# Both parts of every weight tile written by DMAs instead of by ScalarE and VectorE

## The chip, the cores and the metric

One core of a Trainium2 chip runs the whole program. The metric is the device time of one execution in microseconds. Two runs of the kernel before took 2135.54 and 2133.32 us, a median of 2134.43 us.

## The reference

The reference is a decoder trunk of two layers over 512 tokens of width 1024, in float32, with a memory of 256 tokens. Each layer adds, to the running `x`, half of a SwiGLU FFN (inner width 2816), a token mixer, a cross-attention with four heads into the memory, and half of a second FFN. An RMS norm stands ahead of each step and one at the end.

```
x = x + 0.5 * swiglu_ffn(rms_norm(x, ffn1_norm[i]), ...)
x = x + mixer_i(rms_norm(x, mix_norm[i]))
x = x + memory_cross_attention(rms_norm(x, xattn_norm[i]), rms_norm(mem, mem_norm[i]), ...)
x = x + 0.5 * swiglu_ffn(rms_norm(x, ffn2_norm[i]), ...)
```

The mixer of layer 0 is a causal pooling over 2, 4, 8 and 16 positions with a small linear map per channel group. The mixer of layer 1 is a native sparse attention (NSA): 16 heads in 4 groups, with a compressed branch, a selected branch and a sliding window.

## The kernel before

**Number format.** Every product is worked out in float32r, to which a float32 value is rounded first. So that nothing is lost, each operand is held as a pair: a high part, which is the value rounded to float32r, and a low part, which is the value minus the high part. `mm3` (lines 274 to 278) multiplies two pairs with three matmuls: high by high, high by low, low by high. Where the weight is the first operand, the third of these matmuls (L278) is the first that reads its low part; where it is the second operand (the values of the memory and the keys and values of NSA), it is the second one (L277).

**The weights.** All weights, 192 MB, lie in one array in the order of their use, cut into 741 tiles of 128 partitions by at most 512 columns (719 of them full, 256 KB each). A full tile mostly holds four blocks of 128 by 128. Each block is used for one `mm3`, 512 tokens wide in the FFNs, the projections of `x` and the output projections, and 256 memory tokens wide for the keys of the memory (`mem_k`). In `mem_v` a whole tile is one block, used for two `mm3`. The reading side, `take` (from L257), asks at the first block of tile t that `split` has been called for the tiles up to t + AHEAD.

**How a tile is prepared.** `Stream.load` (L235) lets SyncE (SP) load it into a raw buffer. `Stream.split` lets ScalarE (ACT) round it into the high part (L246). `Stream.low` lets VectorE (DVE) subtract the high part from the raw tile (L255); during NSA, from `use_pool` on, GpSimd (POOL) does this for the odd tiles. There are 4 raw buffers and 5 buffers for pairs. A pair's buffer is free when the last matmul of the tile in it has ended.

**Order.** The stages run in the order of the reference. The last output products of one stage run beside the norm and the first products of the next. The memory's norm and preparation run beside the output products of the first FFN; `mem_k`, `mem_v` and the pooling mixer share a stage, and the memory of layer 1 is projected beside the end of NSA. A scheduler orders the instructions on each engine by its own costs, with the calls' order as priority, and adds the semaphore waits. So an engine's order isn't always that of the calls: ACT rounds tiles up to four ahead of their use, and ahead of work that was called earlier. Each engine, and each queue of an engine that issues DMAs, works in its own order.

Of the kernel before, what the change touches and what calls it, by code (L numbers as in the profile page):

```python
# [13 lines left out]
P = 128  # L14
# [29 lines left out]
WT = 512  # L44
# Units of a head's softmax run this many units ahead of their values.
LAG = 3
# Units at which the four steps of the next group's compressed branch are issued (from 16: in the next group).
CMP = (12, 15, 16, 18)
# Units of the last group but one at which a quarter of the memory is prepared.
MP = (12, 13, 14, 15)  # L50
# Where in the k order of the first products a norm is worked out: FFN, cross-attention, NSA (columns, row).
NORMS = (3, 6, 3, 7)
# The pool mixer beside the memory's projections, by step: the norm (a, b), the windows' sums on GpSimd (f) and their
# means (m), or both on the vector engine (n).
HOOKS = "10:a 12:b 16:f4 16:f5 20:n0 24:n1 31:f6 40:n2 42:m4 48:f7 48:n3 58:m5 68:m6 73:m7"
# Products that keep the tensor engine's clock up while the first loads are under way.
WARM = 8
# Steps of other projections done by the end of each unit of a group.
FILL = ([3, 3, 3, 6, 9, 14, 16, 17, 18, 21, 23, 24, 24, 24, 24, 24],
# [138 lines left out]
def plan():  # L198
    """The weights in the order of their use, cut into tiles of up to WT columns."""
    tiles, cur, n, off = [], [], 0, 0  # L200
    for s in all_segs():
        if s is None or n + s[3] > WT:
            tiles.append((cur, off, n))
            off += P * n
            cur, n = [], 0
        if s is None:
            continue
        cur.append(s)
        n += s[3]
    tiles.append((cur, off, n))  # L210
    return tiles, off + P * n
# [6 lines left out]
class Stream:  # L218
    """The weights in the order of their use: each tile is loaded once and split into two float32r
    parts whose sum is the tile exactly."""  # L220

    RAW, HL, AHEAD = 4, 5, 3

    def __init__(self, nc, dram, raw_pool, hl_pool):
        self.nc, self.dram, self.raw_pool, self.hl_pool = nc, dram, raw_pool, hl_pool
        self.where = [(t, j) for t, (segs, _, _) in enumerate(TILES) for j in range(len(segs))]
        self.pos = 0
        self.raw, self.hl = [], []
        self.use_pool = False

    def load(self, n):
        while len(self.raw) < min(n, len(TILES)):
            _, off, w = TILES[len(self.raw)]
            r = self.raw_pool.tile([P, WT], F32, name="wraw")
            self.nc.sync.dma_start(r[:, :w], bass.AP(tensor=self.dram.tensor, offset=self.dram.offset + off,  # L235
                                                     ap=[[w, P], [1, w]]))
            self.raw.append(r)

    def split(self, n):
        while len(self.hl) < min(n, len(TILES)):  # L240
            self.load(len(self.hl) + self.RAW)
            t = len(self.hl)
            w = TILES[t][2]
            pool = self.kept_pool if t >= len(TILES) - KEPT else self.hl_pool
            self.hl.append(pool.tile([P, 2, WT], F32R, name="whl"))
            self.nc.scalar.copy(self.hl[t][:, 0, :w], self.raw[t][:, :w])  # L246
            if t > 0:
                self.low(t - 1)
            if t == len(TILES) - 1:
                self.low(t)  # L250

    def low(self, t):
        w, hl = TILES[t][2], self.hl[t]
        eng = self.nc.gpsimd if self.use_pool and t % 2 else self.nc.vector
        eng.tensor_sub(hl[:, 1, :w], self.raw[t][:, :w], hl[:, 0, :w].bitcast(F32))  # L255

# [12 lines left out]
class Kernel:  # L269
# [10 lines left out]
    def mm4(self, ps, a, b, start, stop, **kw):  # L280
        """Contraction over stacked parts: a holds both parts of one side, b each part of the other."""
        mm = self.nc.tensor.matmul
        mm(ps, a, b[0], start=start, stop=False, **kw)
        mm(ps, a, b[1], start=False, stop=stop, **kw)

    def split(self, hl, src):
        """hl: the pair of float32r parts of src."""
        self.nc.scalar.copy(hl[0], src)
        self.nc.vector.tensor_sub(hl[1], src, hl[0].bitcast(F32))
# [15 lines left out]
    def run(self):  # L305
        tc, nc = self.tc, self.nc
        pool = tc.tile_pool
        with pool(name="const", bufs=1) as const, pool(name="tmps", bufs=5) as self.tmps, \
                pool(name="small", bufs=4) as self.small, pool(name="bc", bufs=1) as self.bc, \
                pool(name="xg", bufs=DK) as self.xgp, \  # L310
                pool(name="raw", bufs=Stream.RAW) as rawp, pool(name="hl", bufs=Stream.HL) as hlp, \
                pool(name="psum", bufs=8, space=bass.MemoryType.PSUM) as self.psum:
            self.const = const
            self.ws = Stream(nc, self.wts, rawp, hlp)
            self.identf = const.tile([P, P], F32, name="identf")
# [47 lines left out]
    def gained(self, k, g):  # L363
        """x[k] * gain as two parts."""
        nc = self.nc
# [7 lines left out]
    def squared(self, k, eng=None):  # L373
        """The share of x[k] in the norm's sum."""
        nc = self.nc
# [8 lines left out]
    def stage_x(self, k, g, eng=None):  # L384
        """What the next norm and its products need of x[k], once it is final."""
        if g is not None:
            if k == 0:
                self.xg = [None] * DK
            self.gained(k, g)
        self.squared(k, eng)  # L390

    def rms_cols(self, sums, nt, tag):
        """1/rms by token as columns [128, nt]."""
        nc = self.nc
# [11 lines left out]
    def spread(self, rcol, nt):  # L406
        """The columns as a row on every partition, in PSUM."""
        pb = self.bank("psb")
# [9 lines left out]
    def rms_row(self, row, hl, more=None):  # L418
        """1/rms by token as a row on every partition, from the parts of its sum (and a further one in float32)."""
        nc = self.nc  # L420
# [19 lines left out]
    def first(self, pss, outs, xs, k0=0, k1=DK, hooks=None):  # L440
        """Several outputs at once, so that the last of xs are needed late."""
        for k in range(k0, k1):
# [73 lines left out]
    def finish(self, outs, hT):  # L516
        """The last products and the final norm; the last output goes by halves of the tokens, so that the first
        half is normalised and stored beside the products of the second."""
        nc = self.nc
# [61 lines left out]
    def mem_norm(self):  # L581
        """The memory by its 1/rms, on every partition."""
        nc = self.nc
# [18 lines left out]
    def mem_prep(self, l):  # L602
        """The normalised memory as two parts."""
        nc = self.nc
# [19 lines left out]
    def mem_k(self, l, hd):  # L624
        """K^T of a head: kT[head] is the pair of parts, [128, chunk of the head's width, key]."""
        nc = self.nc
# [13 lines left out]
    def mem_v(self, l):  # L640
        """V: v[key block][half of the width] is the pair of parts."""
        nc = self.nc
# [18 lines left out]
    def pool_sums(self, k):  # L661
        """x[k] over its rms, and its sums over the trailing window (for a window of two: the token before, and for
        the first token that token itself)."""
        nc, att = self.nc, self.att
# [17 lines left out]
    def pool_means(self, k, h, s, rc, half):  # L682
        """The trailing means minus the token itself, times the gain, as two parts."""
        nc = self.nc
# [174 lines left out]
    def nsa(self, gnext):  # L859
# [62 lines left out]
        def blocks(kv):  # L922
            """The blocks of 32 positions as columns: [position % 2 and channel, position // 2, group and block]."""
            kc = [self.b8("kc").rearrange("p (c n) -> p c n", c=16) for _ in range(2)]
# [48 lines left out]
        def cmp_k(hT):  # L973
            """Keys by group, between columns of zeros."""
            ps = self.bank("psk")
# [13 lines left out]
        def cmp_v(hR, w):  # L989
            """Values by group, with the rows of the other heads' blocks at zero for each head."""  # L990
            w = [[t[:, None, :].to_broadcast([P, 2, P]) for t in wc] for wc in w]
# [170 lines left out]
        def begin(u):  # L1162
            """The scores of a unit, and the softmax of the one before."""
            if 0 <= u - 1 < len(units):
                normalised(*units[u - 1], *pr[u - 1])
            if u < len(units):
                pr[u] = softmax(*units[u])
# [105 lines left out]
def pack(inputs):  # L1273
    """The weights as one array in the order of their use, and the small arrays by partition."""
    mats = {}
# [46 lines left out]
```

## Time and profile before

| | |
|---|---|
| runs shown | 2133.32 and 2135.54 us, median 2134.43 us |
| span of the profiled execution, first to last instruction | 2132.6 us, 1.8 us under the median of the runs; its time outside the span is not shown |
| TensorE matmul (PE) | 2103.2 us busy, 99% of the span |
| VectorE (DVE) | 1186.2 us, 56% |
| ScalarE (ACT) | 916.9 us, 43% |
| GpSimd (POOL) | 237.8 us, 11% |
| DMA | 200.57 MB in all, mean 94 GB/s |

Busy time is the time in which an engine works on an instruction; DMA-issuing instructions are not counted in it. Matmuls overlap, so the time from the start of one to the start of the next tells more than the duration of one. The granted clock of TensorE is in the profile as a share of its full speed, 2.4 GHz.

### The profile page before, as it was taken

The numbers are of one execution on the slowest core, as the hardware profiler recorded it, in microseconds if no ns is written. First come the engines' busy times: TensorE is split into PE (matmuls) and PEld (weight loads), VectorE is DVE, ScalarE is ACT, GpSimd is POOL, SyncE is SP. The second block draws the span as 40 slices with busy tenths as digits, with TensorE's granted clock in tenths as the row PEclk, the third lists the DMA queues.
The fourth block names the chain that finished last, engine by engine and source line by source line (L and its number), as shares of the span: only waits on it lengthen the run. The fifth ranks groups of instructions, "written<-read, shape, count | busy, mean of one in ns | idle before, by whom it ended". The sixth has DMA issues, their size and how long they took to land.

```text
span 2132.6 us, 27926 instructions
## 1 busy us (share of the span) xinstructions
PE 2103.2 (99%) x10144; PEld 1769.6 (83%) x10144; DVE 1186.2 (56%) x2049; ACT 916.9 (43%) x1748; POOL 237.8 (11%) x294
## 2 busy tenths in 40 slices
PE   9999999899999999999999999999999999999998
PEld 6888888788888888888888888888898888888887
DVE  7554444964645453455544336788986555454433
ACT  4333333464533333343333334887876444333332
POOL 2000000511000000000000003544453100000000
PEclk9999999899999999999999999999999999999999
DMA  4333333431333333333333332411224223333332
GB/s 139 109 99 97 116 94 99 121 113 56 96 97 99 97 96 99 94 99 95 98 97 96 99 96 78 129 36 45 61 59 132 86 72 96 95 98 99 95 99 80
DMA packets 111035, 200.57 MB, mean 94 GB/s; under 512 B 12464, under 2 KB 17328, under 8 KB 110896
## 3 DMA queue, kind: packets, MB, share of 16 engines
q1 hardware_dynamic: 110208, 198.20, 31.8%
q8 instruction: 80, 1.31, 0.3%
q10 hardware_dynamic: 688, 0.58, 0.1%
q14 instruction: 59, 0.48, 0.1%
HBM read 196.63 MB, written 2.10 MB: 93 GB/s over the span
## 4 chain that ended last, share of the span: by engine, by line
PE 93%; DVE 3%; ACT 2%; issue 1%; DMA 1%; POOL 0%; DVEq 0%; SPq 0%; ACTq 0%; POOLq 0%
PE psy L277 10%; PE psy L276 10%; PE psy L278 10%; PE psu L277 7%; PE psg L277 7%; PE psg L278 7%; PE psu L278 7%; PE psu L276 7%; PE psg L276 7%; PE pso L1142 2%; PE psq L278 2%; PE psq L277 2%; PE psq L276 2%; PE pst L1130 1%; PE psf L278 1%
## 5 line engine op out<-in xcount | busy, mean ns | idle before, releaser
L246 ACT CAST whl<-wraw 128x512 fp32r<-128x512 f32 (+2 forms) x741 | 455.1, 617 | 901.9 <-PE psy L278 284.1
L255 DVE TENSOR_TENSOR whl<-wraw,whl 128x512 fp32r<-128x512 f32 (+1 forms) x687 | 483.2, 705 | 513.5 <-ACT whl L246 508.3
L276 PE MATMUL psy<-hT,whl 128*128 128x512 f32 (+1 forms) x726 | 278.0, 383 | 0.0
L278 PE MATMUL psy<-hT,whl 128*128 128x512 f32 (+1 forms) x726 | 277.8, 383 | 0.0
L277 PE MATMUL psy<-hT,whl 128*128 128x512 f32 (+1 forms) x726 | 277.8, 383 | 0.0
L277 PE MATMUL psu<-xg,whl 128*128 128x512 f32 x640 | 249.0, 389 | 0.0
L276 PE MATMUL psu<-xg,whl 128*128 128x512 f32 x640 | 249.0, 389 | 0.0
L276 PE MATMUL psg<-xg,whl 128*128 128x512 f32 x640 | 249.0, 389 | 0.0
L278 PE MATMUL psg<-xg,whl 128*128 128x512 f32 x640 | 249.0, 389 | 0.0
L278 PE MATMUL psu<-xg,whl 128*128 128x512 f32 x640 | 249.0, 389 | 0.0
L277 PE MATMUL psg<-xg,whl 128*128 128x512 f32 x640 | 249.0, 389 | 0.0
L255 POOL TENSOR_TENSOR whl<-wraw,whl 128x512 fp32r<-128x512 f32 (+2 forms) x54 | 70.1, 1298 | 849.3 <-ACT whl L246 840.5
L278 PEld LDWEIGHTS psy<-hT,whl 128*128 128x128 f32 x726 | 136.4, 188 | 26.8
L276 PEld LDWEIGHTS psy<-hT,whl 128*128 128x128 f32 x726 | 136.4, 188 | 26.6
L277 PEld LDWEIGHTS psy<-hT,whl 128*128 128x128 f32 x726 | 136.4, 188 | 26.4
L276 PEld LDWEIGHTS psu<-xg,whl 128*128 128x128 f32 x640 | 120.2, 188 | 25.2
L276 PEld LDWEIGHTS psg<-xg,whl 128*128 128x128 f32 x640 | 120.1, 188 | 25.1
L278 PEld LDWEIGHTS psg<-xg,whl 128*128 128x128 f32 x640 | 120.2, 188 | 24.8
L277 PEld LDWEIGHTS psg<-xg,whl 128*128 128x128 f32 x640 | 120.1, 188 | 24.9
L277 PEld LDWEIGHTS psu<-xg,whl 128*128 128x128 f32 x640 | 120.1, 188 | 24.8
L278 PEld LDWEIGHTS psu<-xg,whl 128*128 128x128 f32 x640 | 120.1, 188 | 24.8
L469 DVE TENSOR_TENSOR u<-psu,rbc 128x512 f32<-128x512 f32 x80 | 55.3, 692 | 103.1 <-PE psu L278 103.1
(291 smaller groups left out, 3417.7 us busy)
## 6 DMA issues: line engine op xcount, KB each, us to landing
wraw<-wts SPq DMA_DIRECT2D x719, 256.0 KB, 2.6
wraw<-wts SPq DMA_DIRECT2D x12, 192.0 KB, 2.4
x<-xT SPq DMA_DIRECT2D x8, 256.0 KB, 5.6
mraw<-memT SPq DMA_DIRECT2D x4, 512.0 KB, 4.2
out<-y SPq DMA_DIRECT2D x6, 256.0 KB, 3.6
wraw<-wts SPq DMA_DIRECT2D x8, 152.0 KB, 2.2
out<-y ACTq DMA_DIRECT2D x2, 256.0 KB, 3.6
wraw<-wts SPq DMA_DIRECT2D x2, 128.0 KB, 2.2
```

Of the source, the lines that this page charges most:

```text
L246: self.nc.scalar.copy(self.hl[t][:, 0, :w], self.raw[t][:, :w])
L255: eng.tensor_sub(hl[:, 1, :w], self.raw[t][:, :w], hl[:, 0, :w].bitcast(F32))
L276: mm(ps, a[0], b[0], start=start, stop=False)
L277: mm(ps, a[0], b[1], start=False, stop=False)
L278: mm(ps, a[1], b[0], start=False, stop=stop)
L469: nc.vector.tensor_mul(u, psu, self.rbc)
L1130: nc.tensor.transpose(pt[:, j * P:(j + 1) * P], pr[br][:, j * P:(j + 1) * P], self.identf)
L1142: nc.tensor.matmul(ps[:, c0:c0 + 256], v[br][j][:, g, :], pT[br][:, hl, j, :], start=False, stop=br == 1 and j == 2 * i2 + 1 and hl == 1)
```

## The change

The raw buffers, SP's loads, ACT's rounding copy and the subtraction on DVE and POOL are gone. In their place a DMA issued by POOL loads the tile from float32 into the high part, whose type is float32r. ACT writes the negative of the high part into the low part. A second DMA issued by POOL reads the same tile again and adds it to what stands in the low part (`accum_op`). There are 7 buffers for pairs in place of 5 and 4 raw ones, which is the same memory. `split` keeps 2 tiles ahead in place of 3, and the first DMA of a tile is called 2 further tiles ahead. Everything else, the matmuls too, is as before; the rest of the diff removes comments.

```diff
-    RAW, HL, AHEAD = 4, 5, 3
+    RAW, HL, AHEAD = 3, 7, 2
...
     def load(self, n):
-        while len(self.raw) < min(n, len(TILES)):
-            _, off, w = TILES[len(self.raw)]
-            r = self.raw_pool.tile([P, WT], F32, name="wraw")
-            self.nc.sync.dma_start(r[:, :w], bass.AP(...))
-            self.raw.append(r)
-
-    def split(self, n):
         while len(self.hl) < min(n, len(TILES)):
-            self.load(len(self.hl) + self.RAW)
             t = len(self.hl)
             w = TILES[t][2]
             pool = self.kept_pool if t >= len(TILES) - KEPT else self.hl_pool
             self.hl.append(pool.tile([P, 2, WT], F32R, name="whl"))
-            self.nc.scalar.copy(self.hl[t][:, 0, :w], self.raw[t][:, :w])
-            if t > 0:
-                self.low(t - 1)
-            if t == len(TILES) - 1:
-                self.low(t)
-
-    def low(self, t):
-        w, hl = TILES[t][2], self.hl[t]
-        eng = self.nc.gpsimd if self.use_pool and t % 2 else self.nc.vector
-        eng.tensor_sub(hl[:, 1, :w], self.raw[t][:, :w], hl[:, 0, :w].bitcast(F32))
+            self.nc.gpsimd.dma_start(self.hl[t][:, 0, :w], self.src(t))
+
+    def split(self, n):
+        while self.done < min(n, len(TILES)):
+            self.load(self.done + self.RAW)
+            t = self.done
+            w, hl = TILES[t][2], self.hl[t]
+            self.nc.scalar.mul(hl[:, 1, :w], hl[:, 0, :w].bitcast(F32), -1.0)
+            self.nc.gpsimd.dma_start(hl[:, 1, :w], self.src(t), accum_op=ALU.add)
+            self.done += 1
```

## Rows read from the trace of the kernel before

**Rows 1.** The page's busy times of the engines and the span.
```profile
span 2132.6 us, 27926 instructions
PE 2103.2 (99%) x10144; PEld 1769.6 (83%) x10144; DVE 1186.2 (56%) x2049; ACT 916.9 (43%) x1748; POOL 237.8 (11%) x294
```

**Rows 2.** Waits of PE: who waited for whom, total us, times, longest us.
```profile
PE psv L277 <- DVE whl L255: 5.6, 2, 4.4
PE psk L278 <- DVE whl L255: 4.6, 3, 2.9
PE psf L278 <- DVE whl L255: 2.8, 2, 2.4
```

**Rows 3.** The page's groups of instructions that prepare the weights.
```profile
L246 ACT CAST whl<-wraw 128x512 fp32r<-128x512 f32 (+2 forms) x741 | 455.1, 617 | 901.9 <-PE psy L278 284.1
L255 DVE TENSOR_TENSOR whl<-wraw,whl 128x512 fp32r<-128x512 f32 (+1 forms) x687 | 483.2, 705 | 513.5 <-ACT whl L246 508.3
...
L255 POOL TENSOR_TENSOR whl<-wraw,whl 128x512 fp32r<-128x512 f32 (+2 forms) x54 | 70.1, 1298 | 849.3 <-ACT whl L246 840.5
```

**Rows 4.** ACT's instructions in time, 1002 to 1008 us, in the second layer's first FFN.
```profile
1002.21 0.62 ACT L246 CAST whl<-wraw 128x512 fp32r<-128x512 f32 x1 [1.41 <-PE psu L278]
1004.93 0.62 ACT L246 CAST whl<-wraw 128x512 fp32r<-128x512 f32 x1 [2.10 <-PE psu L278]
1006.91 0.62 ACT L288 CAST hT<-u 128x512 fp32r<-128x512 f32 x1 [1.36 <-DVE u L470]
1007.65 0.62 ACT L246 CAST whl<-wraw 128x512 fp32r<-128x512 f32 x1
```

**Rows 5.** Stretches: PE, PEld, DVE, ACT, POOL busy (count), PEclk, DMA share, GB/s.
```profile
900.00:1100.00 200.00, 200.00 (x884) 165.59 (x883) 101.08 (x146) 72.03 (x114) 0.00 (x0) 1.00 0.34 97
370.86:432.77 61.91, 52.71 (x302) 46.78 (x300) 56.11 (x83) 29.11 (x50) 26.81 (x20) 0.89 0.44 128
```

**Rows 6.** Stretches, L246 alone: ACT busy (count), PEclk, DMA share, GB/s.
```profile
370.00:433.00 63.00, 19.72 (x32) 0.89 0.44 128
1370.00:1600.00 230.00, 24.23 (x40) 1.00 0.17 49
1610.00:1636.00 26.00, 10.69 (x18) 1.00 0.58 178
```

**Rows 7.** A stretch, PE alone: PE busy (count), PEclk, DMA share, GB/s.
```profile
392.00:396.00 4.00, 4.00 (x20) 0.50 0.48 134
```

**Rows 8.** PE's high-by-high matmuls in time, in `mem_k`, then `mem_v`.
```profile
381.16 0.28 PE L276 MATMUL psk<-mg,whl 128*128 128x256 f32 x1
381.52 0.28 PE L276 MATMUL psk<-mg,whl 128*128 128x256 f32 x1
...
421.21 0.39 PE L276 MATMUL psv<-whl,mg 128*128 128x512 f32 x1
421.89 0.39 PE L276 MATMUL psv<-whl,mg 128*128 128x512 f32 x1
```

**Rows 9.** DMA: the whole span's load issues; then 6 to 10 us.
```profile
wraw<-wts SPq DMA_DIRECT2D x719, 256.0 KB, 2.6
DMA to landing us min/median/max: 2.0/2.6/5.7
...
DMA packets 768, 1.40 MB, mean 350 GB/s; under 512 B 84, under 2 KB 84, under 8 KB 768
q1 hardware_dynamic: 768, 1.40, 97.6%
```

**Rows 10.** One DMA issue on SP's queue and two POOL groups, as durations.
```profile
1.25 0.42 SPq L235 DMA_DIRECT2D wraw<-wts  x1
...
L670 POOL TENSOR_TENSOR hp<-x,rbc 128x512 f32<-128x512 f32 x4 | 6.4, 1616 | 8.3 <-ACT rbc L438 8.3
L485 POOL TENSOR_TENSOR sqsum<-x 128x512 f32<-128x512 f32 x1 | 1.0, 1038 | 2.8 <-DMA x<-xT 2.8
```

**Rows 11.** PE in time at the opening: first and last low-part wait.
```profile
6.93 0.62 PE L278 MATMUL psf<-xg,whl 128*128 128x512 f32 x2
...
20.67 0.50 PE L278 MATMUL psf<-xg,whl 128*128 128x512 f32 x1 [2.41 <-DVE whl L255]
```

More of the change, by code (lines that the diff above doesn't have):

```diff
@@ L218, with __init__, src @@
 class Stream:
-    RAW, HL, AHEAD = 4, 5, 3
-    def __init__(self, nc, dram, raw_pool, hl_pool):
-        self.nc, self.dram, self.raw_pool, self.hl_pool = nc, dram, raw_pool, hl_pool
+    RAW, HL, AHEAD = 3, 7, 2
+    def __init__(self, nc, dram, hl_pool):
+        self.nc, self.dram, self.hl_pool = nc, dram, hl_pool
         self.where = [(t, j) for t, (segs, _, _) in enumerate(TILES) for j in range(len(segs))]
         self.pos = 0
-        self.raw, self.hl = [], []
+        self.hl, self.done = [], 0
         self.use_pool = False
+    def src(self, t):
+        _, off, w = TILES[t]
+        return bass.AP(tensor=self.dram.tensor, offset=self.dram.offset + off, ap=[[w, P], [1, w]])
     def load(self, n):
-        while len(self.raw) < min(n, len(TILES)):
-            _, off, w = TILES[len(self.raw)]
-            r = self.raw_pool.tile([P, WT], F32, name="wraw")
-            self.nc.sync.dma_start(r[:, :w], bass.AP(tensor=self.dram.tensor, offset=self.dram.offset + off,
-                                                     ap=[[w, P], [1, w]]))
-            self.raw.append(r)
-    def split(self, n):
         while len(self.hl) < min(n, len(TILES)):
-            self.load(len(self.hl) + self.RAW)
             t = len(self.hl)
@@ L310, in run @@
                 pool(name="xg", bufs=DK) as self.xgp, \
-                pool(name="raw", bufs=Stream.RAW) as rawp, pool(name="hl", bufs=Stream.HL) as hlp, \
+                pool(name="hl", bufs=Stream.HL) as hlp, \
                 pool(name="psum", bufs=8, space=bass.MemoryType.PSUM) as self.psum:
             self.const = const
-            self.ws = Stream(nc, self.wts, rawp, hlp)
+            self.ws = Stream(nc, self.wts, hlp)
             self.identf = const.tile([P, P], F32, name="identf")
```

## The prediction

> **What bounds the kernel now.** I read the busy times first: PE works 2103.2 of 2132.6 us, so all its idle time is 29.4 us, while DVE is at 56% and POOL at 11% [rows 1]. The next view is who PE waits for. Three rows of low parts that DVE had not finished (L255) hold 13.0 us of that idle time [rows 2]. After such a stall the granted clock is the lower level, 1.2 GHz, for some microseconds: 0.50 in a stretch of 4 us [rows 7]. The stretch of `mem_k`, `mem_v` and the pooling mixer shows what this costs: 32 tiles are rounded for it [rows 6]; its 16 tiles of `mem_k` need four blocks of 0.36 us each, its 16 tiles of `mem_v` two of 0.68 us [rows 8], so 16 x 1.44 + 16 x 1.36 = 44.8 us, and it takes 61.9 us at a mean clock of 0.89 [rows 5]. That is a loss of 17.1 us. Elsewhere PE is full: 200.0 us of 200 in an FFN, at clock 1.00, with a DMA share of 0.34 [rows 5].
>
> So DVE's 483.2 us of subtractions [rows 3] are work beside PE. The question is whether two DMAs for each tile keep up with PE. In the FFNs PE takes one tile in 1004.93 - 1002.21 = 2.72 us [rows 4]. This is the budget of POOL's queue and of the DMA engines for a tile.
>
> **What is removed.** 687 subtractions on DVE at 705 ns and 54 on POOL at 1298 ns [rows 3], 553.3 us of busy time, all of it covered by PE except for the waits above. ACT's 741 casts of 617 ns become 741 multiplications of the same shape; ACT has 57% of the span idle [rows 1], so I cost them at nothing. If each took 0.1 us more, that would be 74 us, still under PE. SP's 741 loads go too, and with them SP's wait for a raw buffer. The cost of issuing moves to POOL.
>
> **What is added: DMA work.** With the queue full, the engines move 350 GB/s at 97.6% of their time, so one pass over a tile of 262,144 bytes takes 0.75 us [rows 9]. At the present spacing a pass takes 0.34 x 2.72 = 0.92 us of share [rows 5]. The first DMA is one pass. The accumulating one is not in the trace. At the least it is one pass more, 1.50 us for the tile. It must also read what it adds to: three passes, 2.25 us. With a further pass for writing it is four, 3.0 us, or 4 x 0.92 = 3.68 us at the dearer rate, the upper bound. I take 2.25 us, since the rate of the full queue is nearest to a state in which the engines hardly rest: 83% of 2.72, covered in the FFNs. The Trainium skill, page "Collectives: The Full Stack", section "The bandwidth ceiling: the fold count and why AG ≠ RS ≠ AR", says that an add in the DMA path costs a second source read and not the add itself; by it the tile would be at three passes, 2.25 us, without it 1.50. No row here shows such a transfer.
>
> **What is added: POOL issues.** There are 1482, two per tile. SP spends 0.42 us on one [rows 10], which is the lower bound: 0.84 us for a tile. The upper bound is the slowest POOL operation on a whole tile, 1.62 us, 3.24 us for a tile. I take POOL's fast one, 1.04 us [rows 10], between the two ends: 2.08 us, under the budget. The Trainium skill, page "DMA: Bandwidth & Descriptors", section "Latency and other measured facts", gives about 1 µs to the first byte for a DMA issued by GpSimd and 0.6 for one issued by SP; an estimate of 2 x 1 us from it stays in the budget too. No row here shows one.
>
> **The wait that is added, and its queue.** The accumulating DMA waits on POOL for ACT's negation, and that waits for the first DMA to land. By the order of the calls three tiles' loads are ahead, so the loop from one load over its negation to the next is: landing 2.6 us [rows 9] + 0.62 + two issues at 1.04 = 5.3 us, and the budget of three tiles is 8.2 us. Behind the waiting instruction on POOL are the next loads and, in NSA, the scaling of the probabilities; there only 40 tiles are prepared in 230 us [rows 6], 5.8 us each. Seven pair buffers leave six tiles, 16.3 us, for two landings and a negation, 5.8 us in all, so latency alone is hidden. ACT's order helps: it rounds one tile just before and one just after an FFN activation without losing the beat of 2.72 us [rows 4].
>
> **Where tiles are short, it is not covered.** In the stretch of 61.9 us, with four tiles ready on entry, the stream sets (32 - 4) x 2.25 = 63.0 us: +1.1 us. DVE's backlog no longer matters there, but the stream takes its place. With 1.50 us PE's own 44.8 us remain (-17.1), with 3.0 us it is 84 us (+22). The second `mem_v`, 16 tiles at 1.36 = 21.8 us with 18 casts in its 26 us [rows 6], would take (16 - 4) x 2.25 = 27.0 us: +5.2. At the opening the first low part is used at 6.93 us [rows 11]; now it needs a second landing after the first. One landing of 2.6 us more, against 0.7 us of a subtraction, is about +2 us; a stall of 2.41 us at 20.67 [rows 11] and its slow clock may go in return. I take +2, with bounds of -4 and +6.
>
> **The sum.** 1.1 + 5.2 + 2 = +8.3 us on the span of 2132.6, or 2140.9; the runs' median lies 1.8 us above this span, hence **2143 us**. With two passes the same stages give -17.1 + 0 - 4 = -21: 2113 us.
>
> **The rivals.**
> - **The stream is slower than PE in the FFNs** (slower than before). It decides from 2.72 us a tile on, either by the DMA passes or by POOL's issues. Of the 741 tiles some 640 lie outside the three stretches of rows 6 and the opening. Each 0.1 us above the budget costs 64 us. With 3.0 us: 640 x 0.28 + 22 + (12 x 3.0 - 21.8 = 14) + 6 = +221, 2355 us. With POOL at 3.24 us: 640 x 0.52 + 29 + 17 + 6 = +385, 2519 us. At 3.68: 614 + 41 + 22 + 6 = +683, 2817 us. For it: no row prices either DMA, both issue on one engine, and three passes at the present spacing's 0.92 us are 2.76 us, just above the budget. Against it: the full queue's 350 GB/s, and POOL's idle time in the FFNs (0.00 busy in 200 us [rows 5]).
> - **POOL's queue order** (slower, just). If a landing takes 5.7 us, the longest in the trace [rows 9], the loop of three tiles is 5.7 + 0.62 + 2.08 = 8.4 us, 2.80 a tile: 640 x 0.08 = +51 and the +8, 2194 us. For it: transfers queue behind each other at 83% share. Against it: the median of 2.6 us.
> - **Faster by more than 2%**, under 2092 us: not even 29.4 us of PE's idle time suffice, and the slow clock would have to go as well. Nothing in the rows gives it beyond that.
>
> **Chances.** Covered in the FFNs, 2113 to 2177 us: 0.47, the likeliest. Stream bound: 0.41. Queue order: 0.10. Faster: 0.01; something else: 0.01. What a measurement of this kernel can tell from no change is about 2%, 43 us. So faster 0.01, within 2% 0.48 (0.47 and the near end of the queue's case), slower 0.51. The likeliest case's own range is 2108 to 2177; since slower cases hold half of the chance, the range that should hold 8 in 10 goes up to 2640, about 3.4 us a tile, with some 0.16 above and little below.
>
> **What would show it.** Right: PE still near 99% with a tile per 2.72 us in the FFNs, a DMA share near 0.83, no waits on low parts there, and the stretch with the mixer ending on waits for `whl` by DMA rather than by DVE. Wrong: PE waiting for the second DMA in each FFN tile, at 1.2 GHz after each stall. Then the DMA share tells the rivals apart: near 1, the passes are dearer than 0.75 us; well under 1 with POOL's queue issuing all the time, it is the issues; with POOL waiting for ACT, the order. A share near 0.55 would say two passes.

## The result, and the profile after

The changed kernel took 2632.86 and 2665.11 us, median 2648.99, against 2134.43 before: a ratio of 1.2413, with a 95% interval of 1.2233 to 1.2592. The forecast was 2143 us, so it failed, and the time lies 9 us above the upper end of the range too. The profiled execution is the one of 2632.86 us.

The page of the kernel after (L243 is the first DMA of a tile, L250 the negation, L251 the accumulating DMA):

```profile
span 2631.2 us, 28798 instructions
PE 2282.5 (87%) x10144; PEld 1764.4 (67%) x10144; DVE 722.1 (27%) x1362; ACT 902.3 (34%) x1748; POOL 1208.9 (46%) x1722
...
q0 software_dynamic: 213408, 384.79, 74.7%
...
L251 POOL DMA_DIRECT2D whl<-wts x741 | 656.5, 895 | 1244.5 <-ACT whl L250 1182.2
L250 ACT ACTIVATE whl<-whl 128x512 fp32r<-128x512 f32 (+2 forms) x741 | 463.6, 627 | 1604.7 <-DMA whl<-wts 1543.6
L243 POOL DMA_DIRECT2D whl<-wts x741 | 630.3, 863 | 66.8 <-PE psy L275 28.9
```

Set beside [rows 1]: the span grew by 498.6 us. PE's idle time went from 29.4 to 348.7 us, and its busy time from 2103.2 to 2282.5 us for the same 10144 matmuls; the mean granted clock fell from 0.994 to 0.977, which makes some 37 of these 179 us (an estimate: 2103.2 x (0.994 / 0.977 - 1)); the rest of them is not explained here. DVE lost its subtractions (1186.2 to 722.1 us), and nothing came of that. The weight DMAs hold the engines for 74.7% of the span; that this is not all they can do is seen in runs below, where the share goes up to 1.14. The line that tells the story is L251's: POOL stood idle for 1182.2 us ahead of accumulating DMAs, waiting for ACT.

Waits of the kernel after (who waited for whom, total us, times, longest us):

```profile
ACT whl L250 <- DMA whl<-wts: 1543.6, 636, 6.4
POOL whl L251 <- ACT whl L250: 1182.2, 620, 5.2
...
PE psy L275 <- DMA whl<-wts: 81.5, 118, 2.6
...
PE psu L275 <- DMA whl<-wts: 63.6, 90, 1.7
PE psg L275 <- DMA whl<-wts: 54.8, 79, 2.5
```

Read from below: PE's first matmul that needs a low part (L275, before it was L278) waits for a DMA; the accumulating DMA waits for the negation; the negation waits for the first DMA. All three happen in the FFNs, where [rows 5] had PE full. The same kind of stretch now (PE, PEld, DVE, ACT, POOL busy (count), PEclk, DMA share, GB/s):

```profile
1100.00:1300.00 200.00, 171.94 (x697) 129.65 (x695) 39.26 (x56) 55.69 (x91) 82.94 (x117) 0.97 0.78 153
```

In 200 us there are 697 matmuls where [rows 5] has 884, so a tile takes 2.72 x 884 / 697 = 3.45 us. The DMA share is 0.78, under the 1.02 that `e_order3` reaches below with PE full, so the engines are not what limits. POOL's queue in this stretch shows why (start us, us, engine, line, operation, idle time before it and what ended it):

```profile
1203.31 0.89 POOL L243 DMA_DIRECT2D whl<-wts  x1
1205.02 0.86 POOL L251 DMA_DIRECT2D whl<-wts  x1 [0.83 <-ACT whl L250]
1205.57 0.88 POOL L243 DMA_DIRECT2D whl<-wts  x1
1209.95 0.86 POOL L251 DMA_DIRECT2D whl<-wts  x1 [3.51 <-ACT whl L250]
1210.50 0.89 POOL L243 DMA_DIRECT2D whl<-wts  x1
1211.81 0.86 POOL L251 DMA_DIRECT2D whl<-wts  x1 [0.43 <-ACT whl L250]
1212.36 0.89 POOL L243 DMA_DIRECT2D whl<-wts  x1
1217.01 0.86 POOL L251 DMA_DIRECT2D whl<-wts  x1 [3.77 <-ACT whl L250]
```

And ACT's negations there:

```profile
1209.03 0.63 ACT L250 ACTIVATE whl<-whl 128x512 fp32r<-128x512 f32 x1 [4.30 <-DMA whl<-wts]
...
1210.89 0.63 ACT L250 ACTIVATE whl<-whl 128x512 fp32r<-128x512 f32 x1 [0.72 <-DMA whl<-wts]
1216.09 0.63 ACT L250 ACTIVATE whl<-whl 128x512 fp32r<-128x512 f32 x1 [4.57 <-DMA whl<-wts]
```

Two things are to be seen. First, loads and accumulating DMAs alternate. How far apart they are is told by counting them from the start to 1206 us (POOL busy (count), PEclk, DMA share, GB/s; L243 alone, then L251 alone):

```profile
0.00:1206.00 1206.00, 311.29 (x359) 0.97 0.80 158
```

```profile
0.00:1206.00 1206.00, 315.57 (x357) 0.97 0.80 158
```

The 359th load, at 1205.57 us, was issued right behind the 357th accumulating DMA. So when POOL waits to accumulate into tile c, only one further load, that of c+1, is under way; the load of c+2 stands behind the waiting instruction. In the order of the calls it stands ahead of it; the scheduler's order on POOL is another.

Second, the load that left at 1205.57 us released ACT at 1210.89: 5.3 us, twice the 2.6 us of a load before [rows 9]. Each load follows directly on an accumulating DMA. The loop is thus load, 5.3 us to the negation, 0.63 for it, 0.3 to the next accumulating DMA (1211.81), 0.55 to the next load (1212.36): 6.8 us, in which two tiles are fetched. The neighbouring loop takes 1217.01 - 1209.95 = 7.1 us. Half of it is the 3.45 us for a tile found above.

### The profile page after: what moved, and what is told of

It reads as the page before. It is cut to its first block, busy times and chain, and to the rows that moved or that the text cites. A ratio compares the mean times of both kernels' runs of the same rounds, so it can differ in the third digit from the quotient of the medians.

```text
span 2631.2 us, 28798 instructions
## 1 busy us (share of the span) xinstructions
PE 2282.5 (87%) x10144; PEld 1764.4 (67%) x10144; DVE 722.1 (27%) x1362; ACT 902.3 (34%) x1748; POOL 1208.9 (46%) x1722
## 3 DMA queue, kind: packets, MB, share of 16 engines
q0 software_dynamic: 213408, 384.79, 74.7%
## 4 chain that ended last, share of the span: by engine, by line
issue 46%; POOL 33%; PE 8%; DMA 8%; DVE 2%; ACT 2%; POOLq 0%; SPq 0%; ACTq 0%; DVEq 0%
POOL whl L243 19%; POOL whl L251 12%; DMA whl<-wts 8%; PE pso L1139 1%; ACT whl L250 1%; PE pst L1127 1%; PE psy L275 1%; PE psy L274 1%; PE psy L273 1%; POOL pr L1120 1%; PE psq L275 0%; POOL prx L793 0%; PE psq L273 0%; PE psq L274 0%; POOLq L243 0%
## 5 line engine op out<-in xcount | busy, mean ns | idle before, releaser
L251 POOL DMA_DIRECT2D whl<-wts x741 | 656.5, 895 | 1244.5 <-ACT whl L250 1182.2
L250 ACT ACTIVATE whl<-whl 128x512 fp32r<-128x512 f32 (+2 forms) x741 | 463.6, 627 | 1604.7 <-DMA whl<-wts 1543.6
L243 POOL DMA_DIRECT2D whl<-wts x741 | 630.3, 863 | 66.8 <-PE psy L275 28.9
L275 PE MATMUL psy<-hT,whl 128*128 128x512 f32 (+1 forms) x726 | 297.6, 410 | 82.5 <-DMA whl<-wts 81.3
L275 PE MATMUL psu<-xg,whl 128*128 128x512 f32 x640 | 263.3, 411 | 64.8 <-DMA whl<-wts 63.6
L275 PE MATMUL psg<-xg,whl 128*128 128x512 f32 x640 | 263.9, 412 | 56.4 <-DMA whl<-wts 54.8
L273 PE MATMUL psy<-hT,whl 128*128 128x512 f32 (+1 forms) x726 | 281.5, 388 | 0.0
L274 PE MATMUL psy<-hT,whl 128*128 128x512 f32 (+1 forms) x726 | 280.9, 387 | 0.0
L273 PE MATMUL psu<-xg,whl 128*128 128x512 f32 x640 | 250.3, 391 | 0.9 <-ACT rbc L423 0.9
L273 PE MATMUL psg<-xg,whl 128*128 128x512 f32 x640 | 250.9, 392 | 0.0
L274 PE MATMUL psg<-xg,whl 128*128 128x512 f32 x640 | 250.7, 392 | 0.0
L274 PE MATMUL psu<-xg,whl 128*128 128x512 f32 x640 | 250.2, 391 | 0.0
L275 PEld LDWEIGHTS psy<-hT,whl 128*128 128x128 f32 x726 | 137.3, 189 | 166.9 <-DMA whl<-wts 143.8
L275 PEld LDWEIGHTS psu<-xg,whl 128*128 128x128 f32 x640 | 119.9, 187 | 136.1 <-DMA whl<-wts 114.0
L275 PEld LDWEIGHTS psg<-xg,whl 128*128 128x128 f32 x640 | 120.3, 188 | 127.7 <-DMA whl<-wts 105.7
L286 DVE TENSOR_TENSOR hT<-u,hT 128x512 fp32r<-128x512 f32 x88 | 60.6, 692 | 470.0 <-ACT hT L285 469.8
L467 DVE TENSOR_TENSOR u<-u,g 128x512 f32<-128x512 f32 x88 | 60.6, 692 | 394.0 <-ACT g L465 393.7
L274 PEld LDWEIGHTS psg<-xg,whl 128*128 128x128 f32 x640 | 120.5, 188 | 26.8
```

What stands on the lines that cost most here:

```text
L243: self.nc.gpsimd.dma_start(self.hl[t][:, 0, :w], self.src(t))
L250: self.nc.scalar.mul(hl[:, 1, :w], hl[:, 0, :w].bitcast(F32), -1.0)
L251: self.nc.gpsimd.dma_start(hl[:, 1, :w], self.src(t), accum_op=ALU.add)
L273: mm(ps, a[0], b[0], start=start, stop=False)
L274: mm(ps, a[0], b[1], start=False, stop=False)
L275: mm(ps, a[1], b[0], start=False, stop=stop)
```

## The experiments

Three theories stood against each other. **T1**: POOL's queue order lets only two tiles be on their way, and latency sets the pace. **T2**: two DMAs, one of them adding, are more than the DMA engines can move in 2.72 us. **T3**, named in the first expectation only: POOL's issues take too long.

**Depth of the order.** `e_order3` holds the accumulating DMA of tile c behind the load of c+2, as the calls have it:

```diff
-            self.nc.gpsimd.dma_start(self.hl[t][:, 0, :w], self.src(t))
+            self.last = self.nc.gpsimd.dma_start(self.hl[t][:, 0, :w], self.src(t)).ins
...
-            self.nc.gpsimd.dma_start(hl[:, 1, :w], self.src(t), accum_op=ALU.add)
+            with self.tc.issue_after(self.last):
+                self.nc.gpsimd.dma_start(hl[:, 1, :w], self.src(t), accum_op=ALU.add)
```

> POOL's order is held so that a tile's accumulating DMA is issued behind the load of the second tile after it (in the changed kernel: behind the load of the first). Theory 1, POOL's queue order: a load waits behind an accumulating DMA that waits for a landing of 5.0 us, so two tiles take about 0.9 + 5.0 + 0.6 + 0.5 = 7.0 us; with three tiles in the loop it is 2.4 us a tile, below PE's 2.72, and the time falls to 2150 to 2230 us. Theory 2, the DMA engines: they are busy 0.774 of 3.55 us, 2.75 us for each tile, so the share goes to 0.95 and more, the landing grows with it, and the time stays at 2250 us or above. Theory 3, POOL's issues (0.55 us each, 1.1 of 3.55 us): no change, 2649 us.

Measured: 2225.79 us, a ratio to before of 1.0436 (1.0405 to 1.0466). This one edit of the order takes away 423 of the 515 us. Its FFNs (columns as above), then POOL in them:

```profile
1100.00:1300.00 200.00, 200.00 (x884) 165.68 (x883) 37.98 (x56) 63.37 (x105) 106.98 (x148) 1.00 1.02 194
```

```profile
1203.06 0.55 POOL L244 DMA_DIRECT2D whl<-wts  x1 [1.26 <-PE psy L277]
1203.60 0.91 POOL L253 DMA_DIRECT2D whl<-wts  x1
1205.78 0.55 POOL L244 DMA_DIRECT2D whl<-wts  x1 [1.27 <-PE psy L277]
1207.02 0.87 POOL L253 DMA_DIRECT2D whl<-wts  x1 [0.69 <-ACT whl L251]
```

PE is full again at a clock of 1.00, and POOL's load now waits for PE to free a buffer: the weights are ahead. The same two DMAs for each tile are moved at PE's pace, so T2 falls for the FFNs, and T3 falls with the time. One sign of T2 did come: the share rose to 1.02. But PE is full at it, so a share of 1 was no limit.

`e_order4` is the same with `RAW = 4`, so that the accumulating DMA stands behind the load of c+3.

> As the run before, but behind the load of the third tile after it (one more tile of the seven buffers is loaded ahead). Theory 1: no further gain over three tiles in the loop, 2150 to 2230 us. Theory 2: no further gain either, but a longer landing and a DMA share near 1, 2250 us or more. If the landing grows in proportion to the depth, the engines are the bound; if it stays near 5.0 us, the order was.

Measured: 2218.33 us, 1.0401 (1.0371 to 1.0431), and the FFNs as full as with three. The landings do not grow with the depth: 4.5 us (median) for loads and 5.2 us for accumulating DMAs, as in `e_order3`. Where PE is full, depth beyond three tiles gives nothing; where tiles are short it does, as is shown further down.

`e_order1` goes the other way: each load is held behind the accumulating DMA of the tile before it (and `split` is called four tiles ahead instead of two).

```diff
-    RAW, HL, AHEAD = 3, 7, 2
+    RAW, HL, AHEAD = 1, 7, 4
...
+            if t:
+                self.tc.add_manual_dep(self.last.ins, self.acc.ins.name, ...)
```

> The other end of the order: every load is held behind the accumulating DMA of the tile before it, so one tile is in the loop. Theory 1 (POOL's queue order): one tile takes what two take in the changed kernel, the accumulating DMA's issue 0.54, the load's landing of some 5.2 us behind it, 0.63 for the negation and two handovers of 0.1 to 0.3 us, 6.8 us, so 741 x 6.8 = about 5040 us. Theory 2 (the DMA engines are the bound in the changed kernel): the same traffic, so the time stays near 2650 us.

Measured: 4541.24 us in one run (before, beside it: 2133.27). POOL in an FFN:

```profile
2004.45 0.86 POOL L255 DMA_DIRECT2D whl<-wts  x1 [4.79 <-ACT whl L254]
2005.00 0.88 POOL L244 DMA_DIRECT2D whl<-wts  x1
2010.26 0.86 POOL L255 DMA_DIRECT2D whl<-wts  x1 [4.38 <-ACT whl L254]
```

One tile for each loop of 5.8 us, and 741 x 5.8 = 4298 us; where the other 243 us lie was not traced. T1's figure of some 5040 was too high, since it took a landing of 5.2 us and the loads landed in a median of 4.3 us; T2's 2650 is far off. Four depths, 4541, 2649, 2226 and 2218 us, with the bytes unchanged: T1 is shown.

**What the adding costs.** `e_no_acc` leaves the accumulating DMA out:

```diff
-            self.nc.gpsimd.dma_start(hl[:, 1, :w], self.src(t), accum_op=ALU.add)
```

> The accumulating DMA is left out, so the low part stays the negative of the high part. It prices the loading, casting DMA alone: theory 1 and 2 both expect PE's pace, 2120 to 2150 us; a landing of about 3 us and a DMA share of 0.34 would say that the cast costs no more than the plain load of before, a share of 0.45 that it costs a third more. Theory 3 expects 2130 us as well.

Measured: 2137.69 us in one run (before: 2132.89). Its FFNs:

```profile
900.00:1100.00 200.00, 200.00 (x884) 165.56 (x883) 52.88 (x73) 71.22 (x115) 39.07 (x74) 1.00 0.39 96
```

Loading through a casting DMA on POOL, and the negation on ACT, cost next to nothing in time: some 5 of the 515 us. The share lies between the 0.34 and the 0.45 of the expectation, so the casting load holds the engines somewhat longer than the plain one. The rest of the loss hangs on the second DMA.

`e_plain2` keeps the order of the changed kernel, two tiles, but the second DMA writes instead of adding:

```diff
-            self.nc.gpsimd.dma_start(hl[:, 1, :w], self.src(t), accum_op=ALU.add)
+            self.nc.gpsimd.dma_start(hl[:, 1, :w], self.src(t))
```

> The second DMA writes instead of adding (the low part becomes a second copy of the rounded tile), with the same waits and the same order on POOL's queue. Theory 1: the loop stays, and only the landing changes; at 4 us it is (0.9 + 4 + 0.6 + 0.5) / 2 = 3.0 us a tile, some 2350 us. Theory 2: two casting passes are some 1.85 us a tile, PE's pace, 2150 us. The share gives the price of adding against writing.

Measured: 2184.2 us in one run (before: 2132.89); T1's figure of 2350 failed, and T2's 2150 is nearer. In the FFNs:

```profile
900.00:1100.00 200.00, 200.00 (x884) 165.55 (x884) 50.39 (x70) 69.05 (x114) 78.38 (x148) 1.00 0.78 195
```

T1 did not fail with its figure: a load now lands in a median of 3.2 us, not 4, and with the other terms of the loop above (0.55 + 3.2 + 0.63 + 0.3) / 2 = 2.3 us is under 2.72. But this run alone does not tell T1 from T2, since both allow PE's pace at such a landing; the four depths do. It says that a depth of two is enough with landings of about 3 us. It also gives the prices, as busy time of the engines at 2.72 us a tile: the first DMA takes 0.39 x 2.72 = 1.06 us, a second one that writes (0.78 - 0.39) x 2.72 = 1.06, one that adds (1.02 - 0.39) x 2.72 = 1.71.

**The 92 us that remain with the order mended.** In `e_order3` the stretch with `mem_k`, `mem_v` and the mixer takes 80.5 us instead of 61.9. Its first part (`mem_k`) and second part (`mem_v`):

```profile
376.10:418.10 42.00, 27.70 (x184) 25.87 (x183) 31.54 (x34) 13.06 (x23) 38.25 (x46) 0.88 0.80 153
418.10:456.60 38.50, 27.81 (x111) 18.83 (x109) 8.12 (x18) 13.62 (x23) 24.64 (x34) 0.96 1.05 215
```

The parts differ: in `mem_v` the DMA share is 1.05, in `mem_k` POOL is busy for 38.25 of 42 us while the share is 0.80. POOL in `mem_k`:

```profile
384.14 3.49 POOL L669 TENSOR_TENSOR hp<-x,rbc 128x512 f32<-128x512 f32 x2 [0.79 <-ACT rbc L437]
387.59 1.51 POOL L677 TENSOR_TENSOR hs<-hp 128x527 f32<-128x527 f32 x1
389.05 0.88 POOL L253 DMA_DIRECT2D whl<-wts  x1
389.67 1.36 POOL L677 TENSOR_TENSOR hs<-hs 128x525 f32<-128x525 f32 x1
390.68 0.86 POOL L244 DMA_DIRECT2D whl<-wts  x1
```

The mixer's window sums stand between the DMA issues. `e_o3_mix` is `e_order3` with those sums on DVE:

```diff
-        eng = nc.gpsimd if win > 4 else nc.vector
+        eng = nc.vector
```

> As e_order3, but the windows' sums of the pooling mixer are worked out on DVE instead of POOL, so that POOL's queue holds nothing but DMA issues in mem_k. M1 (the 42 us that mem_k takes in e_order3, against 33 before, come from the mixer's POOL instructions standing between the DMA issues): mem_k takes 33 to 37 us, its stretch has a DMA share near 1 throughout, and the whole is 5 to 9 us faster than e_order3, about 2218. M2 (the stretch is set by what the DMA engines can move): nothing changes, or it gets slower where DVE's added 14 us delay the mixer; mem_k stays at 42 us, about 2226. In both, mem_v stays at 38 us, since there POOL had no work of the mixer already.

Measured: 2210.08 us, 1.0359 (1.0341 to 1.0376), 15.7 us less than `e_order3`. Its `mem_k` and `mem_v`:

```profile
375.10:411.40 36.30, 30.36 (x206) 28.82 (x204) 19.69 (x44) 13.43 (x24) 20.63 (x29) 0.86 1.01 205
411.40:444.10 32.70, 23.73 (x87) 14.91 (x87) 13.76 (x29) 13.31 (x24) 20.13 (x28) 1.00 1.08 223
```

M1 is shown for `mem_k`: it takes 36.3 us at a share of 1.01. The gain on the whole, 15.7 us, is more than the 5 to 9 that M1 gave, and that `mem_v` fell from 38.5 to 32.7 us was expected by neither. The issues tell most of it: `e_order3` issues 12 accumulating DMAs in `mem_k` and 16 in `mem_v`, `e_o3_mix` 14 and 14. Two tiles fewer were left for `mem_v`, at 38.5 / 16 = 2.4 us each, an estimate of 4.8 of the 5.8 us.

Two more places are the start of NSA (from the first to the last matmul of `psh` 34.5 us before, 55.7 in `e_order3`) and the second `mem_v` (1681.80 to 1714.40 below). First the start of NSA before, then both places in `e_order3`, then both in `e_order4`:

```profile
1326.90:1361.40 34.50, 30.32 (x171) 25.61 (x170) 21.43 (x43) 25.96 (x56) 16.29 (x14) 0.95 0.52 158
```

```profile
1362.00:1417.70 55.70, 37.39 (x173) 28.85 (x173) 12.30 (x31) 26.21 (x55) 35.30 (x50) 0.88 1.00 200
1681.80:1714.40 32.60, 25.51 (x101) 17.07 (x100) 3.36 (x5) 11.49 (x19) 20.32 (x29) 1.00 1.08 228
```

```profile
1368.20:1416.70 48.50, 35.58 (x176) 25.89 (x175) 12.19 (x31) 25.55 (x54) 35.58 (x51) 0.96 1.10 227
1680.10:1709.90 29.80, 25.67 (x99) 16.93 (x98) 3.36 (x5) 11.89 (x20) 21.66 (x30) 1.00 1.14 251
```

In `e_order3` 228 GB/s is 2 x 262,144 bytes in 2.30 us for a tile. That looks like T2, engines that are full, but it is not their limit: with one tile more under way the same places move 227 and 251 GB/s, 2.09 us for a tile in the second. In the second `mem_v` POOL waits in `e_order3` for ACT ahead of 14 accumulating DMAs, in `e_order4` mostly for PE to free a buffer (waits of POOL: total us, times, longest us; `e_order3`, then `e_order4`):

```profile
POOL whl L253 <- ACT whl L251: 12.0, 14, 1.7
```

```profile
POOL whl L244 <- PE psv L277: 6.4, 12, 1.2
```

So with three tiles the order still sets the pace where tiles are short: 3 x 2.30 = 6.9 us, as long as the loop of the changed kernel (in the second `mem_v` POOL's accumulating DMAs start at 1686.08 and, three tiles on, at 1693.02 us). What limits with four (the engines at a share of 1.14, or the seven buffers) was not separated, so T2 is not shown anywhere. That `e_order4` is only 7.5 us faster on the whole has to do with a loss ahead of these places: its `mem_k` starts at 384.3 us, in `e_order3` at 376.1; why was not traced.

The four places make 5.2 (up to `mem_k`) + 18.6 + 21.2 + 10.7 = 55.7 of the 89.6 us by which the span of `e_order3` exceeds that of before; the other 34 us lie between them and behind the last and were not traced.

**Half of the change.** `e_sp_load` keeps SP's load and ACT's rounding copy, and replaces only DVE's subtraction by a negation and an accumulating DMA, so that no load stands in POOL's queue:

```diff
-        eng.tensor_sub(hl[:, 1, :w], self.raw[t][:, :w], hl[:, 0, :w].bitcast(F32))
+        self.nc.scalar.mul(hl[:, 1, :w], hl[:, 0, :w].bitcast(F32), -1.0)
+        self.nc.gpsimd.dma_start(hl[:, 1, :w], ..., accum_op=ALU.add)
```

> Only the subtraction is replaced: SP loads the raw tile and ACT rounds it, as in the kernel before (4 raw buffers, 5 pairs), ACT then negates and POOL issues the accumulating DMA alone. No load stands behind a wait on POOL. Theory 1: PE's pace in the FFNs, with the losses of the short-tile stages left, 2170 to 2240 us. Theory 2: a plain load at 0.92 us and an accumulating DMA at 1.71 us are 2.63 us of the engines' time per tile, so no better than the runs with the order held, 2220 us or more. POOL should be busy about 0.9 us per tile, and the landing of the accumulating DMA, alone on its queue, 3 to 4 us.

Measured: 2202.14 us, 1.0321 (1.0302 to 1.034), in T1's range and under T2's 2220. Its FFNs:

```profile
1100.00:1300.00 200.00, 200.00 (x884) 165.67 (x883) 35.38 (x52) 109.59 (x178) 63.38 (x74) 1.00 0.94 194
```

They are full without any edit of the order; the losses are again where tiles are short (the stretch with the mixer takes 77.2 us, from 375.6 to 452.8). The accumulating DMA lands in a median of 4.4 us, more than the 3 to 4 expected. The wait in the queue goes as well when the loads are on another queue.

**A version that would be faster than before?** `hyb` is the kernel before, and only the odd ones of the 32 tiles of the stretch with the mixer get their low part as in `e_sp_load`.

> The kernel before, in which only the odd ones of the 32 tiles of the first mem_k and mem_v stretch get their low part from a negation and an accumulating DMA; there VectorE's backlog costs 17.1 us. If the backlog is what counts, the stretch of 61.9 us loses 5 to 15 us and the time is 2118 to 2130 us. If the DMA engines take over (0.92 + 1.71 / 2 = 1.78 us a tile, 57 us for 32), it gains 5 us at most; if the accumulating DMAs land too late for the five pair buffers, it is slower than before by up to 10 us.

Measured: 2143.22 us, 1.0044 (1.003 to 1.0058), so 0.4% slower, the third case of the expectation; the stretch takes 73.1 us instead of 61.9. PE waits for the second DMA (waits of PE):

```profile
PE psk L284 <- DMA whl<-wts: 13.6, 3, 5.2
PE psv L283 <- DMA whl<-wts: 3.5, 2, 2.3
```

`b_mix` is the kernel before with the mixer's sums on DVE, the edit of `e_o3_mix` alone.

> The kernel before, with the mixer's windows' sums on DVE instead of POOL; the weights are prepared by SP, ACT and DVE as before. In its trace a subtraction of a low part takes 1.5 to 1.8 us while POOL adds up windows, and 0.68 us while POOL does nothing. D1 (DVE is late in this stretch because it is slowed beside POOL): with POOL quiet, DVE does the 14 us of sums in addition and is still done earlier; the stretch of 61.9 us comes to 45 to 54 us, the waits for low parts there go, and the whole is 8 to 17 us faster than before, 2117 to 2125. D2 (DVE is late because it has too much to do): 14 us more make the stretch longer by up to 14 us, 2134 to 2148.

Measured: 2132.12 us, 0.9992 (0.9983 to 1.0001): no difference that the runs tell. D1's mechanism is there (a subtraction in this stretch took 27.52 / 32 = 0.86 us on average before and takes 22.63 / 33 = 0.69 now), but the sums that came in used up what it freed: between the same two times DVE is busy for 54.33 us of 61.9, against 56.11 [rows 5]. The stretch takes 60.4 us, so neither D1's 45 to 54 us nor D2's longer stretch came, and PE still waits 9.5 us there for low parts from DVE (9.0 before).

`b_mixhyb` and `b_mixq` add the accumulating DMA to `b_mix`, for every second and every fourth of the 32 tiles.

> As b_mix, but the odd ones of the 32 tiles of the stretch with the mixer get their low part by a negation on ACT and an accumulating DMA, as in hyb; POOL's queue holds nothing else there. DVE drops from 54 to 43 us in a stretch whose products need 44.8. V1 (hyb was late because the mixer's sums stood in POOL's queue): the stretch comes from 60.4 down to 48 to 53 us, the whole to 2120 to 2125, faster than before by 0.4 to 0.6%. V2 (an accumulation lands too late for five pair buffers anyway, 4.1 to 4.9 us after its issue): PE waits for DMA as in hyb, and the whole stays at 2130 to 2145.

> As b_mixhyb, but only every fourth of the 32 tiles gets its low part by the accumulating DMA. DVE drops by 5.5 us only. V1: the stretch comes to 53 to 57 us, the whole to 2124 to 2130. V2: each of eight accumulations is waited for once, by about 1 us, and the gain on DVE is lost: 2130 to 2138.

Measured: 2137.94 us, 1.0023 (1.0014 to 1.0033), and 2133.83 us, 1.0003 (0.9994 to 1.0013). V1 falls: the stretch takes 65.1 and 62.3 us, and with POOL's queue empty of other work `mem_k` still waits, in `b_mixhyb` longest for DVE's subtractions (8.5 us, one of 6.0), and `mem_v` for the DMA (3.2 us). Both times lie in V2's ranges, but its wait for the DMA is the smaller one, so V2 is not shown either. No version was found that beats the kernel before.

## Why the prediction was wrong

**What bounds the kernel: right for the FFNs, in part for the stretch with the mixer.** Without the accumulating DMA the kernel has 458 us less work on DVE (728.3 us) and runs in 2137.69 us: that work was worth nothing. ACT's 741 negations take 627 ns against 617 for the casts [rows 3]; costing them at nothing was right. But the 17.1 us that I put down to DVE's backlog do not go with it: in `e_no_acc`, where DVE subtracts no weights, the stretch takes 57.0 us (372.7 to 429.7), not 44.8, and PE waits there for a load (3.3 us) and for negations (3.9 us). No run came near 44.8 us, so what else holds the stretch stays open.

**The failed step: "By the order of the calls three tiles' loads are ahead".** The engine's order is not that of the calls; the document said so of ACT, and I did not apply it to POOL. It was two tiles, so the loop was not covered and set the pace, 3.45 us for a tile. In the same step I took 2.6 us as the landing, from loads that run beside no second stream. Behind accumulating DMAs it was 5.2 us (median of all loads after). My own formula shows that it took both: two tiles with 2.6 us give (2.6 + 0.62 + 2.08) / 2 = 2.65 us, under the budget; three tiles with 5.2 us give 7.9 / 3 = 2.63, under it too; two with 5.2 give 3.95. The measured pace is 3.45, since an issue is cheaper than I took it: with 0.55 us for each the same sum is (5.2 + 0.62 + 1.1) / 2 = 3.46. `e_order3` mends the one and `e_plain2` the other, and in each the FFNs are full.

**The rival "POOL's queue order" had the mechanism and not the size.** It used the longest landing and three tiles, 2.80 us for a tile and 2194 us; with two tiles the same sum would have been 4.2 us. The sign that I named for it (POOL waiting for ACT, at a DMA share well under 1) is what the trace shows. It had a chance of 0.10; the stream that is slower than PE, at 0.41, is not what made the loss in the FFNs.

**DMA passes: a little too dear, and the share was misread.** I took 2.25 us for a tile. The 2.30 of `e_order3` is near it by luck, since there the order still sets the pace; `e_order4` does a tile in 2.09, so the engines need no more than that. Nor is the adding DMA two passes of the load, as the sum had it: by busy time at PE's pace it takes 1.71 us and the load 1.06. I expected a share of 0.83 in the FFNs, and it is 1.02 with PE still full; it goes up to 1.14, so a share of 1 did not mean that no more could be moved. The Trainium skill, page "Collectives: The Full Stack", section "The bandwidth ceiling: the fold count and why AG ≠ RS ≠ AR", says of the reducing step of a ring that an add costs the second source read. The runs agree that there is such a cost, of less than a full pass: 1.71 us of the engines for the DMA that adds against 1.06 for the one that writes.

**POOL's issues: too dear.** I took 1.04 us. Behind either kind the next instruction starts 0.54 to 0.55 us later (1205.02 to 1205.57 above, 1203.06 to 1203.60 in `e_order3`), though the accumulating one is shown with 0.86. This erred on the safe side.

**The stages with short tiles: too cheap.** I gave the stretch with the mixer +1.1 us; with the order mended it is +18.6. Most of that goes with POOL's own work in the queue, since without it the stretch takes 36.3 + 32.7 = 69.0 us, +7.1: the 26.81 us of that work stand in [rows 5], and I counted what waits behind POOL in NSA but not here. For the second `mem_v` I took +5.2 and it is +10.7 (from the last matmul of `psk` to that of `psv` 21.4 us before, 32.1 in `e_order3`): 32.1 us at 2.30 are 14 tiles, so two were ready on entry and not four, as `AHEAD = 2` has it; and I took the stream to be bound by the engines, where `e_order4` needs 29.8 us. The opening, +2 by me, is +5.2 by the start of `mem_k`. The start of NSA, +21.2 us, was not in the sum: I had looked at the 40 tiles of the 230 us behind it, while this stage rounds 25 tiles in its 34.5 us and reads 158 GB/s already in the trace of before, against 97 in an FFN [rows 5].

**Range and chances.** Half of the chance lay on slower, and the upper end was drawn at about 3.4 us for a tile. It was 3.45, and the short stages came on top.

## What to carry to other kernels

An instruction that issues a DMA and waits holds up every later load on its queue, so read the order on that queue, not in the source, and count how many tiles are under way when it waits: pace is loop time over that number. Take the landing time from transfers that share the engines as they will after the change; here it doubled. A DMA share near 1 does not by itself say that the engines are the limit: try one tile more under way. The remedy for the wait can be an order with one tile more in flight (2649 to 2226 us) or a second queue for the loads (2202 us); here both stayed slower than before, since an engine that was not on the path gives nothing back when it is relieved.

## What the runs showed of the hardware that was not expected

- **Landing depends on what is moved beside a load.** A load of 256 KB by a casting DMA lands in a median of 2.9 us where no second DMA is issued (`e_no_acc`), 3.2 beside a second one that writes, 4.3 to 5.2 behind one that adds. Beside adding DMAs on another queue (`e_sp_load`) SP's plain load lands in 3.6 us, against 2.6 before. So the shared engines make part of the delay; how much the shared queue makes is not shown. The Trainium skill, page "DMA: Bandwidth & Descriptors", section "Anatomy of one DMA — SWDGE (gpsimd) path", gives 2.0 µs and the bytes at 436 GB/s, an estimate of 2.6 us for this tile: near the 2.9 us, half of the 5.2.
- **DVE slows down beside POOL.** In the kernel before, with POOL adding up windows, DVE in time:

```profile
382.51 1.49 DVE L255 TENSOR_TENSOR whl<-wraw,whl 128x512 fp32r<-128x512 f32 x1
383.92 1.54 DVE L688 TENSOR_TENSOR pp<-hp 128x512 f32<-128x512 f32 x1
...
398.23 0.68 DVE L255 TENSOR_TENSOR whl<-wraw,whl 128x512 fp32r<-128x512 f32 x1
```

  From 382.05 us on POOL was in two sums of 2.86 us together, at 398 us it was idle. The same subtraction takes 1.49 and 0.68 us. In `e_o3_mix` DVE is busy for 33.45 us in `mem_k` and `mem_v` together, against 39.66 in `e_order3`, although all the sums were moved to it. The Trainium skill, page "SBUF — State Buffer", section "Who interferes with whom", says that a DVE instruction with two inputs in SBUF contends with a GpSimd instruction that reads SBUF; these rows agree, at some 0.8 us for each such instruction.
